# Layer-norm squares summed on VectorE, a group's squares issued one step earlier, and four low-part subtractions moved from GpSimd to VectorE

## The chip, the cores and the metric

One core of a Trainium2 chip runs the whole program. The metric is device time in microseconds (us): a launch from start to end, the median of several runs. The engines are named as in the profile: PE is the matrix engine (TensorE), DVE is VectorE, ACT is ScalarE, POOL is GpSimd, SP issues most of the DMA transfers. Each engine works through its own list of instructions in order and waits where an instruction needs a result that is not there yet.

## The reference, cut to what matters

The program is one inference step of a hybrid decoder on 336 tokens (8 running sequences of 8 tokens, 16 learned tokens, a prompt of 256), all in float32, with 1024 features. Two branches read one input projection, and a large expert layer follows:

```
xn   = rmsnorm(x);  proj = xn @ w_in + b_in          # 80 column blocks of 128
u    = ga * sigmoid(gb)                              # conformer branch
c    = silu(layernorm(causal_depthwise(u, 31 taps)))
y_a  = c @ w_conf_out + b_conf_out
xs, B, C, dt = ...                                   # Mamba-2 branch, 8 groups of 4 heads
y    = ssd(xs, dt, B, C, state) + D * xs
y    = group_rmsnorm(y * silu(z))                    # mean of squares per group
y_b  = y @ w_m_out
x    = x + (sigmoid(g_a) * y_a + sigmoid(g_b) * y_b) @ w_o
x    = x + peer(rmsnorm(x))                          # 16384 experts, 16 per head and token
```

Two of these steps are touched: the variance of the layer norm (a sum of squares over 1024 features, of which 128 lie on the partitions and 8 are tiles side by side) and the squares of each group for the grouped norm.

## The kernel before, in words

Activations lie with features on the 128 partitions and tokens along the row: a tile of 128 features by 336 tokens, eight tiles for 1024 features. Float32 products are formed from a high and a low part. `weight` (L234 to L243) loads a block of 128 x 1024 weights by DMA into `wraw`, ACT casts it to the high part `wh` (L211), and a subtraction `wraw - wh` gives the low part `wl` (L212). Which engine subtracts is set by a share `lm[0]`: with 0.05 one weight in twenty goes to DVE and the others to POOL. `proj` then runs 16 matmuls with `wh` and 8 with `wl`. There are two buffers each for `wh` and `wl`.

The first part of the program is a loop over eight groups `g`. In the turn of group `g + 1` the 128-column blocks of that group are projected, and between these projections the generator `ssd` of the group before is advanced, one `yield` at a time, so that its small matmuls lie between the large ones. Matmuls of this part are pinned: PE runs them in the order in which the code issues them. The other engines' orders are chosen by the scheduler at build time. The last steps of `ssd` are `update(0)`, `update(2)` (state sums, written back to HBM in `ssm_s`), and then the squares: two on ACT (L634), their sum on POOL (L635), a matmul `pgn` that sums over partitions, and an addition on DVE (L641).

In the turn of the last group (g = 7) the tasks are eight gate projections, the gates 0 to 7 below. After gate 0 comes `norm_mean` (L703): PE sums the convolution outputs, ACT scales the mean `rs` (L707), DVE subtracts it from eight tiles (L709), ACT squares them (L711) and POOL adds seven of them to the first (L713). Then comes gate 1, and behind it the `pgn` matmul of group 6. `norm_scale` (L717) follows gate 3: PE sums `squares[0]` over partitions, and `rstd_of` (L201 to L208, on DVE and ACT) makes the reciprocal root. After gate 7 the `conf_out` projections 0 to 7 use the normalised result, with other work between them: the squares of group 7 and, behind `conf_out(1)`, `gnorm_stats`, which turns the eight groups' sums into one bf16 operand on DVE (L201 to L222, tile `acs`). The matmuls `pgb` behind `conf_out(5)` spread this operand over the partitions, and DVE scales each group with it (L657).

After that come the projections with `w_m_out` and `w_o`, the query projection, the choice of experts, and two long loops over 128 blocks each of the two expert tables (L1180 and L1271), during which rows are also gathered one token at a time (L994).

Of the kernel before, what the change touches and what calls it, by code (L numbers as in the profile page):

```python
# [13 lines left out]
OP = mybir.AluOpType  # L14
# [31 lines left out]
HB = 64  # L46
KTILES = ((0, NGAT), (128, 128), (256, 64))
NU = (54, 28, 40)
LM = (0.05, 0.05, 0.1, 0.5)
CE = 1  # L50
LOW = 400
NW0 = 3
# [80 lines left out]
def body(tc, ia, oa, stop=None):  # L133
    nc = tc.nc
    with ExitStack() as top:
# [10 lines left out]
        def mm(*a_, **kw):  # L146
            i_ = nc.tensor.matmul(*a_, **kw)  # L147
            if pin[0]:
                tc.keep_in_program_order(i_)
# [26 lines left out]
        def V(name, j):  # L176
            o, n = VEC[name]
            return vec[:, o + j:o + j + 1]

        def C(name, rows=128):  # L180
            o, n = CST[name]
            if o < NCK:
                return cst[:rows, o:o + n]
            return cstm[0][:rows, o - NCK:o - NCK + n] if o < NCM else cstm[1][:rows, o - NCM:o - NCM + n]
# [6 lines left out]
        def act(out, in_, f, **kw):  # L191
            chain(nc.scalar.activation(out, in_, f, **kw))  # L192

        def pj(name="pj"):
            return ps.tile([128, PJ], F32, name=name, tag="pj", bufs=3)[:, :T]

        def rstd_of(dst, p, n, pool, tag="yo", load=True):
            r, c_ = dst.shape
            v = pool.tile([128, c_], F32, name="rsv", tag=tag, bufs=2)[:r]
            t = pool.tile([128, c_], F32, name="rst", tag=tag, bufs=2)[:r]  # L200
            nc.vector.tensor_scalar(v, p, 1.0 / n, EPS, op0=OP.mult, op1=OP.add)  # L201
            if load:
                chain(nc.scalar.preload_act_table_set("natural_log_exp_and_others"))
            act(t, v, AF.Ln)
            act(t, t, AF.Exp, scale=-0.5)
            nc.vector.scalar_tensor_tensor(v, v, -0.5, t, op0=OP.mult, op1=OP.mult)
            nc.vector.tensor_tensor(v, v, t, op=OP.mult)
            nc.vector.scalar_tensor_tensor(dst, v, 1.5, t, op0=OP.add, op1=OP.mult)  # L208
# [5 lines left out]
        def stack3(dst, src, n, pool, tag):  # L214
            r_ = pool.tile([128, T], F32, name="s3r", tag=tag, bufs=2)[:n]
            b_ = pool.tile([128, 2 * T], BF, name="s3b", tag=tag, bufs=2)[:n, :T]
            nc.vector.tensor_copy(dst[:n], src)
            nc.vector.tensor_tensor(r_, src, dst[:n], op=OP.subtract)
            nc.vector.tensor_copy(dst[H:H + n], r_)
            nc.vector.tensor_copy(b_, r_)  # L220
            nc.vector.tensor_tensor(r_, r_, b_, op=OP.subtract)
            nc.vector.tensor_copy(dst[2 * H:2 * H + n], r_)  # L222
# [4 lines left out]
        def proj(out, w, act, first=True, last=True):  # L227
            for k in range(KD):
                for c_ in range(2):
                    mm(out, w[0][:, k, :], act(k)[c_], start=(first and k == 0 and c_ == 0), stop=False)  # L230
            for k in range(KD):
                mm(out, w[1][:, k, :], act(k)[0], start=False, stop=(last and k == KD - 1))

        def weight(src, i):  # L234
            raw = wp.tile([128, KD, 128], F32, name="wraw", bufs=rb[0])
            nc.sync.dma_start(raw, src[i].rearrange("p (k m) -> p k m", m=128))
            h = wp.tile([128, KD, 128], F32R, name="wh", bufs=2)
            l = wp.tile([128, KD, 128], F32R, name="wl", bufs=2)
            nw[0] += 1
            f_ = lm[0]  # L240
            on_dve = int((nw[0] + 1) * f_) > int(nw[0] * f_)
            split(h, l, raw, on_pool=not on_dve, on_dve=lm[0] == 1)
            return h, l  # L243

        lm, nw = [LM[3]], [NW0]

# [3 lines left out]
        def misc(shape, name):  # L250
            return ps.tile(shape, F32, name=name, tag="misc", bufs=2)
# [240 lines left out]
        def ssd(g, xg, bc, sz):  # L492
            BT, CT = bc[:, 0, :], bc[:, 1, :]
            st = sp.tile([128, NQ, 256], F32, name="st", bufs=2)
# [89 lines left out]
            def update(q):  # L584
                pair_ = [misc([128, 512], "pst2"), ps.tile([128, PJ], F32, name="pst2", tag="pj", bufs=3)]
                for d_ in range(2):
                    for s_ in range(2):
                        t_ = slice(32 * s_, 32 * s_ + 32)
                        mm(pair_[s_][:, d_ * 256:(d_ + 1) * 256], Bm[t_, q + d_], wx[0][t_], start=True, stop=True)
                for s_ in range(2):  # L590
                    sv = st[:, 4 * s_ + q:4 * s_ + q + 2].rearrange("p q c -> p (q c)")
                    nc.vector.tensor_tensor(sv, sv, pair_[s_], op=OP.add)
# [33 lines left out]
            yield  # L626
            update(0)
            yield
            update(2)
            nc.sync.dma_start(oa["ssm_s"][g], st)  # L630
            yield
            sq = [tp.tile([128, T], F32, name="sq", bufs=4) for _ in range(2)]
            for b in range(2):
                nc.scalar.activation(sq[b], xg[:, b, :], AF.Square)  # L634
            nc.gpsimd.tensor_tensor(sq[0], sq[0], sq[1], op=OP.add)  # L635
            p = pj("pgn")[:G]
            mm(p, C("gsel")[:, g * G:(g + 1) * G], sq[0], start=True, stop=True)
            if g == 0:
# [5 lines left out]
        def gnorm_stats():  # L644
            r8 = tp.tile([128, T], F32, name="rs", bufs=2)[:G]
            rstd_of(r8, pgn, 256, tp, load=False)
            r24 = mp.tile([3 * H, T], BF, name="acs3", tag="acs3")
            nc.vector.memset(r24, 0.0)
            stack3(r24, r8, G, tp, "yo")
            return r24  # L650

        def gnorm(g, r24):
            p = ps.tile([128, T], F32, name="pgb", tag="y", bufs=2)
            mm(p, id3[:, g:g + 1].to_broadcast([3 * H, 128]), r24, start=True, stop=True)
            for b in range(2):
                y = ygf[g][:, b, :]
                nc.vector.scalar_tensor_tensor(y, y, V("m_norm", 2 * g + b), p, op0=OP.mult, op1=OP.mult)  # L657

        def gsplit(g):
            yh = pair(F32R, "yh")  # L660
            yl = m2.tile([128, 2, T], F32R, name="yl", bufs=8)
            for b in range(2):
                split(yh[:, b, :], yl[:, b, :], ygf[g][:, b, :], on_pool=b == 0)
            yg.append((yh, yl))
# [27 lines left out]
        def conf_out(j):  # L692
            ga = gates[j]
            act(ga, ga, AF.Sigmoid)
            w = weight(ia["w_co"], j)
            p = pj()
            proj(p, w, lambda k: (ch[:, k, :], cl[k]))
            nc.vector.scalar_tensor_tensor(ga, p, V("b_co", j), ga, op0=OP.add, op1=OP.mult)

        gates, squares, normed, r24 = [], [], [], []  # L700

        def norm_mean():
            pm = pj()  # L703
            mm(pm, ones, csum, start=True, stop=False)
            mm(pm, ones, cb[:, KD - 1, :], start=False, stop=True)
            mu = tp.tile([128, T], F32, name="rs", bufs=2)
            nc.scalar.mul(mu, pm, 1.0 / D)  # L707
            for k in range(KD):
                nc.vector.tensor_tensor(cb[:, k, :], cb[:, k, :], mu, op=OP.subtract)  # L709
                sq = tp.tile([128, T], F32, name="sq", bufs=4)  # L710
                nc.scalar.activation(sq, cb[:, k, :], AF.Square)  # L711
                if k:
                    nc.gpsimd.tensor_tensor(squares[0], squares[0], sq, op=OP.add)  # L713
                else:
                    squares.append(sq)

# [31 lines left out]
        for f in steps + zsteps:  # L748
            f()
        lm[0] = LM[0]  # L750
        pin[0] = True
        old = iter(())
        for g in range(G):
            new = ssd(g, *tiles, sz)
            if g + 1 < G:
                tiles, steps = xbc(g + 1)
                tasks = conf(g + 1) + steps
            else:
                lm[0] = LM[1]
                tasks = [gate] * 8  # L760
# [25 lines left out]

        m2 = mix.enter_context(tc.tile_pool(name="m2", bufs=1))
        r24.append(gnorm_stats())
        for j in range(2, 6):
            conf_out(j)  # L790
        for g in range(G):
            gnorm(g, r24[0])
            gsplit(g)
            if g % 2 and g < 4:
                conf_out(6 + g // 2)
        for _ in range(3):
            gate()
        pin[0] = False
        lm[0] = LM[2]
        mh = m2.tile([128, KD, T], F32R, name="mh")  # L800
# [15 lines left out]
        for j in range(KD):  # L816
# [11 lines left out]
            else:  # L828
                sq = tp.tile([128, T], F32, name="sq", bufs=4)
# [575 lines left out]
```

## Time and profile before

| | us |
|---|---|
| median of three runs (lowest to highest) | 1414.23 (1413.54 to 1415.16) |
| the profiled execution's own time | 1416.98 |
| its span in the trace | 1415.2 |
| busy: PE, DVE, POOL, ACT | 1327.6, 1011.0, 596.1, 526.2 |
| mean granted PE clock | 0.977 |

The trace counts from the start of the span. Groups 0 to 7 are projected until about 365 us. The gates, the layer norm, `conf_out` and the grouped norm fill 365 to 465 us, the output and query projections 465 to 640 us, and the expert layer the rest. A row of the timeline has a start, a duration, the engine, the line, the operation with its tiles, and in brackets how long the engine was idle before and what ended that. A row of the table by stretches has for each engine its busy time, then the granted PE clock (1.00 is full speed), the DMA share and GB/s. A row of the chain of waits has a start, a length and the work that the end of the program hung on at that time.

### The profile page before, as it was taken

The page shows a single profiled execution, that of the slowest core. Times are in us where ns is not written, and L with a number is a line of the kernel's source. Part 1 is how long each engine was busy: PE and PEld are TensorE (multiplying, and loading weights), DVE is VectorE, ACT ScalarE, POOL GpSimd, SP SyncE. Part 2 cuts the span into 40 slices and gives each one's busy share as a digit, 9 for nine tenths or more (in the row PEclk, how much of TensorE's full clock was granted, in tenths as well). Part 3 has the DMA queues.
Part 4 walks back from the last instruction along what each step waited for, and adds up shares of the span by engine and source line. Part 5 has one row for each costly group of instructions (what it writes and reads, how often), then busy time and mean ns, then how long its engine had stood idle before and what let it go on. Part 6 is the DMA issues. An engine that isn't in the chain of part 4 may idle for free.

```text
span 1415.2 us, 24492 instructions
## 1 busy us (share of the span) xinstructions
PE 1327.6 (94%) x9294; PEld 1257.4 (89%) x9294; DVE 1011.0 (71%) x2326; ACT 526.2 (37%) x1348; POOL 596.1 (42%) x490
## 2 busy tenths in 40 slices
PE   5899999999699999999999879999979999987997
PEld 3898889888588999989999879999979999987997
DVE  6787778877556434679999966777888787775423
ACT  4678776778564543533222221112110110111001
POOL 2267767767665755743212342223232222242100
PEclk9899999999899999999999999999989999999999
DMA  5435453445324344636999899999999999999983
GB/s 198 149 122 167 165 173 127 151 163 169 120 66 147 124 144 141 201 97 216 416 414 413 322 416 413 381 372 394 408 399 416 373 373 392 388 416 415 414 323 98
DMA packets 86806, 382.05 MB, mean 270 GB/s; under 512 B 10112, under 2 KB 15360, under 8 KB 66080
## 3 DMA queue, kind: packets, MB, share of 16 engines
q1 hardware_dynamic: 64144, 226.87, 44.7%
q0 software_dynamic: 20736, 151.00, 26.3%
q10 hardware_dynamic: 1808, 2.60, 0.5%
q8 instruction: 73, 1.20, 0.3%
q14 instruction: 45, 0.37, 0.1%
HBM read 367.41 MB, written 13.03 MB: 269 GB/s over the span
## 4 chain that ended last, share of the span: by engine, by line
PE 75%; DVE 13%; DMA 8%; ACT 2%; issue 1%; POOL 1%; DVEq 0%; SPq 0%; POOLq 0%; ACTq 0%
PE pj L147 31%; PE va L1271 19%; PE pj L1180 11%; PE pg L1209 4%; DMA eraw<-in_vE_dram 3%; DMA eraw<-in_uT_dram 3%; PE pst L147 2%; DVE ygat L1114 2%; DVE wuv L1106 2%; PE po L147 1%; PE pdec L147 1%; PE py L147 1%; PE ptr L152 1%; DMA nd<-x1d 1%; DVE si L916 1%
## 5 line engine op out<-in xcount | busy, mean ns | idle before, releaser
L994 POOL DMA_INDIRECT wuv<-in_peer_uv_dram,gid x144 | 184.1, 1279 | 510.9 <-DVE ygat L1114 193.0
L212 POOL TENSOR_TENSOR wl<-wraw,wh 128x1024 fp32r<-128x1024 f32 x115 | 276.6, 2406 | 185.4 <-ACT wh L211 111.7
L1180 PE MATMUL pj<-nd,eraw 128*128 128x176 f32 x2048 | 324.1, 318 | 13.3 <-DMA eraw<-in_uT_dram 10.0
L1180 PEld LDWEIGHTS pj<-nd,eraw 128*128 128x128 f32 x2048 | 311.3, 193 | 17.2 <-ACT S L1182 8.3
L1271 PE MATMUL va<-S,eraw 128*128 128x176 f32 x2048 | 314.9, 314 | 11.8 <-DMA eraw<-in_vE_dram 11.8
L1271 PEld LDWEIGHTS va<-S,eraw 128*128 128x128 f32 x2048 | 306.1, 190 | 16.4 <-DMA eraw<-in_vE_dram 14.7
L147 PE MATMUL pj<-ah,wh 128*128 128x336 f32 (+1 forms) x768 | 248.3, 332 | 2.4 <-ACT xnf L192 2.1
L147 PE MATMUL pj<-al,wh 128*128 128x336 f32 (+1 forms) x768 | 239.8, 320 | 0.0
L1114 DVE SCALAR_TENSOR_TENSOR ygat<-wuv,scg,ygat 128x1024 f32<-128x1024 f32 x128 | 164.0, 1281 | 56.0 <-ACT scg L1109 55.1
L1106 DVE SCALAR_TENSOR_TENSOR wuv<-wuv,x2m 128x1024 f32<-128x1024 f32 x128 | 156.1, 1219 | 37.7 <-DMA wuv<-in_peer_uv_dram,gid 37.7
L211 ACT CAST wh<-wraw 128x1024 fp32r<-128x1024 f32 x128 | 134.2, 1049 | 130.3 <-PE pj L147 79.0
L1108 ACT ACTIVATE scg<-scg 128x1 f32<-128x1 f32 x144 | 29.1, 202 | 402.7 <-DVE wuv L1106 391.8
L390 DVE SCALAR_TENSOR_TENSOR pcv<-ccat,vec,pcv 128x272 f32<-128x272 f32 x464 | 152.4, 393 | 18.0 <-ACT pcv L388 18.0
L147 PEld LDWEIGHTS pj<-ah,wh 128*128 128x128 f32 x768 | 147.1, 192 | 10.7 <-ACT xnf L192 3.9
L147 PEld LDWEIGHTS pj<-al,wh 128*128 128x128 f32 x768 | 147.1, 192 | 1.1 <-DVE al L212 0.5
L147 PE MATMUL pj<-ah,wl 128*128 128x336 f32 (+1 forms) x768 | 138.2, 318 | 0.0
L147 PEld LDWEIGHTS pj<-ah,wl 128*128 128x128 f32 x768 | 122.5, 188 | 0.8 <-issue 0.7
L1182 ACT ACTIVATE S<-pj 128x176 f32<-128x176 f32 x128 | 37.6, 311 | 156.0 <-PE pj L1180 155.9
L1209 PE MATMUL pg<-oh 128*128 128x64 bf16 x1056 | 75.5, 241 | 0.0
L1209 PEld LDWEIGHTS <-oh 128*128 128x128 bf16 x1056 | 71.1, 117 | 2.2
L1216 DVE TENSOR_TENSOR S<-S,pg 128x192 f32<-128x192 f32 (+1 forms) x66 | 31.7, 508 | 52.1 <-PE pg L1209 50.4
L405 DVE SCALAR_TENSOR_TENSOR pj<-mcat,vec,pj 128x360 f32<-128x360 f32 x96 | 57.0, 594 | 1.4 <-ACT pj L403 1.1
(353 smaller groups left out, 1704.4 us busy)
## 6 DMA issues: line engine op xcount, KB each, us to landing
eraw<-in_uT_dram SPq DMA_DIRECT2D x128, 512.0 KB
eraw<-in_vE_dram SPq DMA_DIRECT2D x128, 512.0 KB
wraw<-in_w_in_dram SPq DMA_DIRECT2D x80, 512.0 KB
st<-in_state_dram SPq DMA_DIRECT2D x8, 1024.0 KB
out_ssm_s_dram<-st SPq DMA_DIRECT2D x8, 1024.0 KB
wraw<-in_w_mo_dram SPq DMA_DIRECT2D x16, 512.0 KB
wraw<-in_w_q_dram SPq DMA_DIRECT2D x16, 512.0 KB
wraw<-in_w_co_dram SPq DMA_DIRECT2D x8, 512.0 KB
```

Source lines behind the costliest of these rows:

```text
L147: i_ = nc.tensor.matmul(*a_, **kw)
L211: (nc.vector.tensor_copy if on_dve else nc.scalar.copy)(h, src)
L212: (nc.gpsimd if on_pool else nc.vector).tensor_tensor(l, src, h.bitcast(F32), op=OP.subtract)
L390: t = nc.vector.scalar_tensor_tensor(o, i_, wv, a_, op0=OP.mult, op1=OP.add)
L405: nc.vector.scalar_tensor_tensor(o, cat[:, w:w + n], wv, o, op0=OP.mult, op1=OP.add)
L994: i_ = nc.gpsimd.indirect_dma_start(out=u, out_offset=None, in_=ia["peer_uv"], in_offset=bass.IndirectOffsetOnAxis(ap=gid[:, c:c + 1], axi ...
L1106: nc.vector.scalar_tensor_tensor(u[:, :D], u[:, :D], 1.0, x2m if c < NPICK else x2e, op0=OP.mult, op1=OP.mult, accum_out=w)
L1114: nc.vector.scalar_tensor_tensor(a_, u[:, D:], scg[:, c:c + 1], a_, op0=OP.mult, op1=OP.add)
L1180: i_ = nc.tensor.matmul(p[:, :ND], raw[:, k, :], nd[:, k, :], start=(k == 0), stop=(k == KD - 1))
L1182: nc.scalar.activation(Sv(b), p[:, :ND], AF.Gelu)
L1209: i_ = nc.tensor.matmul(pg[:, q, :], B[:, q // 4, :, q % 4], A[:, c_, q // 4, :, q % 4], start=(c_ == 0), stop=(c_ == 2))
L1271: i_ = nc.tensor.matmul(va[k // 2][:, k % 2], raw[:, k, :], Sv(b), start=False, stop=(b == 127), skip_group_check=True)
```

## The change

Three edits. The seven additions of the layer norm's squares go from POOL to DVE. In `ssd` the squares of a group and their sum are issued ahead of `update(2)`, in the same step as its state copy to HBM, and no longer one step later; the `pgn` matmul stays where it was on PE. And during `conf_out(2)` to `conf_out(5)` the share of low parts on DVE is 0.999, which is all four; before, it was 0.05, and by the count one of the four was on DVE already.

```diff
-LM = (0.05, 0.05, 0.1, 0.5)
+LM = (0.05, 0.05, 0.1, 0.5, 0.999)
...
             yield
             update(0)
             yield
-            update(2)
-            nc.sync.dma_start(oa["ssm_s"][g], st)
-            yield
             sq = [tp.tile([128, T], F32, name="sq", bufs=4) for _ in range(2)]
             for b in range(2):
                 nc.scalar.activation(sq[b], xg[:, b, :], AF.Square)
             nc.gpsimd.tensor_tensor(sq[0], sq[0], sq[1], op=OP.add)
+            update(2)
+            nc.sync.dma_start(oa["ssm_s"][g], st)
+            yield
             p = pj("pgn")[:G]
             mm(p, C("gsel")[:, g * G:(g + 1) * G], sq[0], start=True, stop=True)
...
                 if k:
-                    nc.gpsimd.tensor_tensor(squares[0], squares[0], sq, op=OP.add)
+                    nc.vector.tensor_tensor(squares[0], squares[0], sq, op=OP.add)
...
         r24.append(gnorm_stats())
+        lm[0] = LM[4]
         for j in range(2, 6):
             conf_out(j)
+        lm[0] = LM[1]
```

The orders of the built programs differ at few places. For groups 0 to 5 the squares stand where they stood on every engine. PE's order differs only in the loop over the first expert table, where at three places a run of 8 to 24 projection matmuls stands one to about 36 `pg` matmuls earlier or later, and DVE's and ACT's lists follow with a few rows.

POOL in the turn of the last group, from the end of group 6's output to the state scaling. Before (`wl` is a weight's low part, L713 the layer norm's sum, L635 the sum of group 6's squares, `wx` the scaled inputs of group 7):

```order
L582 TENSOR_TENSOR xg<-xg,sz 128x336
L212 TENSOR_TENSOR wl<-wraw,wh 128x1024 x2
L530 TENSOR_TENSOR wx_4562<-xt_4559,wd_202 80x256
L212 TENSOR_TENSOR wl<-wraw,wh 128x1024
L713 TENSOR_TENSOR sq<-sq 128x336 x7
L635 TENSOR_TENSOR sq<-sq 128x336
L530 TENSOR_TENSOR wx_4660<-xt_4657,wd_226 128x256
L530 TENSOR_TENSOR wx_4669<-xt_4666,wd_242 128x256
L212 TENSOR_TENSOR wl<-wraw,wh 128x1024
L562 TENSOR_TENSOR st<-st,el 128x256 x8
```

and with the change (the sum of group 6's squares is now L632):

```order
L582 TENSOR_TENSOR xg<-xg,sz 128x336
L212 TENSOR_TENSOR wl<-wraw,wh 128x1024
L632 TENSOR_TENSOR sq<-sq 128x336
L212 TENSOR_TENSOR wl<-wraw,wh 128x1024
L530 TENSOR_TENSOR wx_4567<-xt_4564,wd_202 80x256
L212 TENSOR_TENSOR wl<-wraw,wh 128x1024
L530 TENSOR_TENSOR wx_4660<-xt_4657,wd_226 128x256
L530 TENSOR_TENSOR wx_4669<-xt_4666,wd_242 128x256
L212 TENSOR_TENSOR wl<-wraw,wh 128x1024
L562 TENSOR_TENSOR st<-st,el 128x256 x8
```

The seven additions have left POOL, and the sum of group 6's squares stands three rows of weights and inputs earlier, behind the first of three low parts.

DVE at the same place, with the change, from the mean's subtraction (L709) to the reciprocal root of the layer norm (L201); before, the same rows stood there without the three of L713, and the memset (L648) behind the two rows of L527:

```order
L709 TENSOR_TENSOR cbuf<-cbuf,rs 128x336 x8
L641 TENSOR_TENSOR pgn<-pgn 8x336
L713 TENSOR_TENSOR sq<-sq 128x336
L648 MEMSET acs_5114 96x168
L527 TENSOR_TENSOR xt_4657<-ptr,dtok_218 128x256
L527 TENSOR_TENSOR xt_4666<-ptr,dtok_234 128x256
L713 TENSOR_TENSOR sq<-sq 128x336 x4
L540 TENSOR_TENSOR dec<-dec,pcb 80x4x80
L713 TENSOR_TENSOR sq<-sq 128x336 x2
L540 TENSOR_TENSOR dec<-dec,pcb 128x4x128
L548 COPY hs_4773<-pst 128x256
L201 TENSOR_SCALAR rsv<-pj 128x336
```

The first addition stands behind the addition of group 6's `pgn`, and the last two behind the product with `pcb`, a matmul that PE runs after gate 2.

DVE at `gnorm_stats`, from the sum of group 7's `pgn` to the operand of `pgb`. Before:

```order
L641 TENSOR_TENSOR pgn<-pgn 8x336
L201 TENSOR_SCALAR rsv<-pgn 8x336
L206 SCALAR_TENSOR_TENSOR rsv<-rsv,rst 8x336
...
L217 CAST acs_5114<-rs 8x336
L218 TENSOR_TENSOR s3r<-rs,acs_5114 8x336
L698 SCALAR_TENSOR_TENSOR ge<-pj,vec,ge 128x336
L219 CAST acs_5114<-s3r 8x336
L220 CAST s3b<-s3r 8x336
L221 TENSOR_TENSOR s3r<-s3r,s3b 8x336
L222 CAST acs_5114<-s3r 8x336
```

and with the change:

```order
L641 TENSOR_TENSOR pgn<-pgn 8x336
L201 TENSOR_SCALAR rsv<-pgn 8x336
L212 TENSOR_TENSOR wl<-wraw,wh 128x1024
L206 SCALAR_TENSOR_TENSOR rsv<-rsv,rst 8x336
...
L217 CAST acs_5114<-rs 8x336
L698 SCALAR_TENSOR_TENSOR ge<-pj,vec,ge 128x336
L212 TENSOR_TENSOR wl<-wraw,wh 128x1024
L218 TENSOR_TENSOR s3r<-rs,acs_5114 8x336
L219 CAST acs_5114<-s3r 8x336
L220 CAST s3b<-s3r 8x336
L221 TENSOR_TENSOR s3r<-s3r,s3b 8x336
L698 SCALAR_TENSOR_TENSOR ge<-pj,vec,ge 128x336
L222 CAST acs_5114<-s3r 8x336
```

The low parts of `conf_out(4)` and `conf_out(5)` now stand inside this sequence (that of `conf_out(2)` stands a little ahead of it and that of `conf_out(3)` was there before), and the evictions L698 have moved by a row. On POOL five low parts in a row behind the sum of group 7's squares have become two, those of `conf_out(6)` and `conf_out(7)`.

## The prediction

> **What bounds the kernel now.** I read three views, from coarse to fine. First the page's chain that ended last, which says whose work the end hangs on, and the table by stretches, which says where that holds.
>
> ```profile
> PE 75%; DVE 13%; DMA 8%; ACT 2%; issue 1%; POOL 1%; DVEq 0%; SPq 0%; POOLq 0%; ACTq 0%
> ```
>
> ```profile
> 370.00:390.00 20.00, 8.80 (x44) 6.14 (x43) 5.78 (x14) 9.91 (x27) 12.54 (x12) 0.70 0.33 106
> ...
> 430.00:450.00 20.00, 17.30 (x110) 16.35 (x109) 13.59 (x14) 12.21 (x16) 10.66 (x5) 0.99 0.54 178
> 450.00:470.00 20.00, 17.34 (x94) 16.48 (x94) 15.74 (x29) 9.67 (x20) 12.90 (x10) 0.84 0.26 86
> 470.00:520.00 50.00, 50.00 (x327) 50.00 (x326) 14.66 (x13) 22.45 (x31) 29.24 (x14) 1.00 0.46 143
> ...
> 900.00:1000.00 100.00, 100.00 (x824) 99.22 (x822) 76.00 (x115) 19.45 (x76) 25.62 (x21) 1.00 0.99 388
> 1200.00:1300.00 100.00, 88.17 (x628) 85.15 (x627) 70.38 (x94) 12.94 (x52) 29.59 (x23) 1.00 1.00 406
> ```
>
> The first busy column is PE. It is full from 470 us on until DVE and then the DMA engines (shares 0.99 and 1.00) take over in the expert layer. All of that begins with results of the stages ahead, so time won before 465 us moves the rest forward whole. The hole is at 370 to 390 us, with PE busy for 8.80 of 20 us, in the stage that the change edits. Then PE's waits from 355 to 640 us (total, times, longest), the two longest:
>
> ```profile
> PE pgn L147 <- POOL sq L635: 11.2, 1, 11.2
> PE pgb L147 <- DVE acs L222: 3.4, 1, 3.4
> ```
>
> Last, the timeline at the first of them, PE, then POOL, then ACT:
>
> ```profile
> 373.83 1.40 PE L147 MATMUL pj<-ah,wl 128*128 128x336 f32 x8
> 386.43 1.29 PE L147 MATMUL pgn<-sq,cstm 128*8 128x336 f32 x2 [11.20 <-POOL sq L635]
> ```
>
> ```profile
> 375.37 3.49 POOL L212 TENSOR_TENSOR wl<-wraw,wh 128x1024 fp32r<-128x1024 f32 x1 [3.68 <-ACT wh L211]
> 378.82 6.71 POOL L713 TENSOR_TENSOR sq<-sq 128x336 f32<-128x336 f32 x7
> 385.49 0.89 POOL L635 TENSOR_TENSOR sq<-sq 128x336 f32<-128x336 f32 x1
> ```
>
> ```profile
> 383.62 0.48 ACT L634 ACTIVATE sq<-xg 128x336 f32<-128x336 f32 x1 [0.49 <-POOL sq L713]
> ```
>
> PE ends gate 1 at 375.23 and then needs the squares of group 6. Their sum is queued on POOL behind a low part and the seven additions of the layer norm, and the squares themselves on ACT behind those of the layer norm, which wait for POOL to free a buffer.
>
> **Term 1: the wait for group 6's squares goes, 13.6 us.** With the change the sum stands behind one low part, ahead of `norm_mean`:
>
> ```profile
> 360.99 0.91 POOL L582 TENSOR_TENSOR xg<-xg,sz 128x336 f32<-128x336 f32 x1
> 362.97 2.37 POOL L212 TENSOR_TENSOR wl<-wraw,wh 128x1024 fp32r<-128x1024 f32 x1 [1.07 <-PE pj L147]
> ```
>
> Its input is complete at 361.9, the low part ends at 365.3, and the sum at 0.9 us is there by 366.3, 9 us before PE asks. What the same PE work takes without a wait stands in the chain at group 5's squares, up to `pq` of group 6, against `pq` of group 7 and the norm's matmul now:
>
> ```profile
> 331.85 0.66 PE pgn L147 x2
> ...
> 333.72 3.91 PE pj L147 x24
> 337.63 1.00 PE pq L147 x16
> ...
> 394.65 1.00 PE pq L147 x16
> ...
> 400.55 0.78 PE pj L147 x2
> ```
>
> From `pgn` to `pq` it was 337.63 - 331.85 = 5.78 us there; here it is 394.65 - 375.23 = 19.42 us from the end of gate 1. The difference, 13.6, is the wait of 11.2 and 2.4 us of work done at the half clock that follows it (granted 0.70 in this stretch). The other operands are ready: gate 2's low part was made before, and gate 3's ends at 375.37 + 3.49 = 378.86, ahead of its use. Bounds: 11.2, if the clock fell for another reason, and 13.6.
>
> **Term 2: the additions on DVE, a loss of 0.3 us.** PE needs `squares[0]` 5.90 us after `pq` starts (400.55 - 394.65), so now at 381.01 + 5.90 = 386.9. Before, the sum was ready at 385.5 for a use at 400.5; that cover is gone. DVE has no such addition in the trace. The nearest row is a subtraction of two 128x336 tiles in SBUF, 0.51 us:
>
> ```profile
> L212 DVE TENSOR_TENSOR ml<-gs,mh x4: 507/508/510, 490.1 to 555.6; 128x336 fp32r<-128x336 f32 x4
> ```
>
> Seven cost 3.6 us, where DVE is nearly idle. But a DVE operation on two SBUF tiles waits while POOL is in one, as `rs` did, at 2.58 us here and 0.52 at the program's start (chain, third row):
>
> ```profile
> 405.34 2.58 DVE L208 SCALAR_TENSOR_TENSOR rs<-rsv,rst 128x336 f32<-128x336 f32 x1
> 405.15 2.40 POOL L212 TENSOR_TENSOR wl<-wraw,wh 128x1024 fp32r<-128x1024 f32 x1 [0.21 <-ACT wh L211]
> 16.92 0.52 DVE rs L208
> ```
>
> So I put the list of front's second DVE block on the clock, with POOL's pieces:
>
> ```profile
> 373.22 3.44 DVE L709 TENSOR_TENSOR cbuf<-cbuf,rs 128x336 f32<-128x336 f32 x8 [2.22 <-ACT rs L707]
> 389.39 1.25 POOL L530 TENSOR_TENSOR wx<-xt,wd 128x256 f32<-128x256 f32 x2 [3.01 <-DVE xt L527]
> 397.12 4.62 POOL L562 TENSOR_TENSOR st<-st,el 128x256 f32<-128x256 f32 x8
> ```
>
> L709 ends at 376.7, the `pgn` addition at 377.2. Addition 1 waits for gate 3's low part (378.9) and ends at 379.4; `xt` takes until 380.2; additions 2 and 3 let one L530 (0.6) pass each, until 382; number 4 may meet gate 4's low part, until 384.2; 5 lets one L562 (0.58) pass, 385.2; then the product with `pcb`, and 6 and 7 with an L562 each, 387.2. That is 0.3 late. Bounds: no loss, if POOL's pieces fall between, and 4.8 us, if two more low parts of 2.4 get ahead.
>
> **Term 3: the layer norm's root, a loss of 0.4 us.** POOL's state scaling and the low parts of gates 5 and 6 come some 0.4 us later against PE, since additions get between. The root's three steps meet them as now, and PE's wait behind them grows from 1.00 to 1.4:
>
> ```profile
> 410.37 0.70 PE L147 MATMUL pst<-wx,xt 128*128 128x256 f32 x2 [1.00 <-DVE dec L540]
> ```
>
> Bounds: the wait vanishes (gain 1.0), or one more low part is in the way (loss 2.4).
>
> **Term 4: low parts on DVE, a gain of 0.5 us.** The wait of 3.4 us at `pgb` is this (DVE, POOL, ACT, PE, and from the chain the projection behind it):
>
> ```profile
> 442.72 2.57 DVE L219 CAST acs<-s3r 8x336 bf16<-8x336 f32 x1
> ...
> 450.33 0.33 DVE L222 CAST acs<-s3r 8x336 bf16<-8x336 f32 x1
> 442.70 7.24 POOL L212 TENSOR_TENSOR wl<-wraw,wh 128x1024 fp32r<-128x1024 f32 x3 [3.84 <-ACT wh L211]
> 441.58 1.98 ACT L211 CAST wh<-wraw 128x1024 fp32r<-128x1024 f32 x2
> 446.15 1.05 ACT L211 CAST wh<-wraw 128x1024 fp32r<-128x1024 f32 x1 [2.59 <-issue]
> 450.71 0.72 PE L147 MATMUL pgb<-acs,id 96*128 96x336 bf16 x2 [3.41 <-DVE acs L222]
> 451.43 6.07 PE pj L147 x24
> ```
>
> Three small DVE steps (0.3 to 0.5 us alone, as L222) each wait out one POOL low part of 2.4 us. The change takes the first of the three, that of `conf_out(5)`, and puts it into DVE's list instead, at 1.22 us (half of POOL's 2.40 above):
>
> ```profile
> L212 DVE TENSOR_TENSOR wl<-wraw,wh x13: 1204/1223/1866, 14.1 to 643.6; 128x1024 fp32r<-128x1024 f32 x13
> ```
>
> Cast by 442.6, it ends at 443.8, L218 at 444.3. Then POOL, whose weight 6 is cast at 443.6, takes its turn to 446.5, L219 waits, L220 and L221 end at 447.6. Weight 7 is cast at 447.2, so POOL's last low part starts about 447.6, while DVE evicts L698, and L222 waits for it until 450.2, against 450.7 now: 0.5 us gained. PE is at `pgb` at 447.3, so a wait of 2.9 stays. Bounds: nothing, and 5.8: the whole 3.4, with the 2.4 us by which the projection behind it (6.07) exceeds 3.7 us at full clock. The low part of `conf_out(2)` delays two state sums by 1.3 us, which only the copy to HBM waits for; that of `conf_out(4)` fills a gap in which DVE waits for ACT. What stands behind costs nothing on PE.
>
> [...]
>
> ```profile
> 609.66 0.33 PE L899 MATMUL px<-cst,xe 128*128 128x128 f32 x1 [2.48 <-POOL xe L897]
> 613.00:616.00 3.00, 3.00 (x12) 3.00 (x13) 3.00 (x20) 0.30 (x2) 0.00 (x0) 0.50 0.03 5
> ```
>
> So at 2.9 I keep the half clock.
>
> **Term 5: the expert loops, 0.** Three runs of matmuls moved there; PE and DMA are full either way (900 to 1000 us). Bounds: 2 us to each side.
>
> **Sum.** 13.6 - 0.3 - 0.4 + 0.5 = 13.4 us. The profiled execution took 1416.98, of which 1415.2 are its span; it would take 1403.6. The median of the runs lies 2.75 under it: 1400.8 us.
>
> **The rivals.** (a) The root of the group norm gets through: L219 to L222 pass between POOL's low parts and PE does not wait at `pgb`. Then term 4 is 5.8 and the time 1395.5. For it: POOL has two low parts left for four steps. Against it: both are cast at just the wrong moments. Chance 0.22.
>
> (b) The wait at `pgb` stays near 2.9 but the clock does not fall: 2.4 more, 1398.4. [...] Chance 0.07, since the shorter wait at 609 us did halve it.
>
> (c) A new wait at the norm's matmul: the additions lose the turn to two more low parts, 4.5 us more than in term 2, and the half clock costs 2.4: 1407.7. For it: my list ends within 0.3 us of the need. Against: only two low parts are due there. Chance 0.08.
>
> (d) Slower. The moved runs in the first expert loop break the rhythm of table blocks, gathers and `pg`, and the DMA engines, the bound from 800 to 1300 us, run at 388 GB/s in place of 406: 500 x (406/388 - 1) = 23 us, so 1424. It turns the result once it costs 16.2 us, 3.2% of these 500. Against it: three runs only, and both rates occur in the loops already. Chance 0.03.
>
> (e) The change does nothing on the clock: the wait only changes its place, to another operand behind `pgn`. 1414. I see no operand that is late there. Chance 0.03.
>
> **How the numbers follow.** The forecast has 0.57; its own range is 1398.5 to 1403.5, from terms 2, 3 and 5. With (a) and (b) that makes 0.86 between 1394 and 1405, which is the range. What this measurement can tell from no change is about 0.2%, 2.8 us: faster are the forecast, (a), (b) and (c), 0.94; the same (e), 0.03; slower (d), 0.03.
>
> **What would show it.** In the new profile PE should have no wait at group 6's `pgn`, `pq` of group 7 should start near 381 us, and the granted clock from 370 to 390 should be 1.00. The norm's matmul near 387 shows term 2: a wait there for DVE's L713 of over 1 us makes it (c). L222 should still end some 2.9 us after `conf_out(5)`; if PE does not wait at `pgb`, it is (a). From `pgb` to the end the span should keep its length within 2 us; if it grows by more than 16, it is (d). A `pgn` wait of 5 us or more would make the prediction wrong.

## The result and the profile after

| us | before | changed |
|---|---|---|
| median of four runs (lowest to highest) | 1414.42 (1413.54 to 1415.16) | 1401.87 (1398.62 to 1403.79) |
| ratio, with its 95% interval | | 0.9909 (0.9893 to 0.9925) |
| the profiled execution's own time | 1416.98 | 1403.79 |
| its span | 1415.2 | 1402.0 |
| mean granted PE clock | 0.977 | 0.982 |

The forecast was 1400.8, with a range from 1394 to 1405. The profiled executions lie 13.2 us apart, the medians 12.55; the sum of the terms was 13.4. In the changed kernel the sum of a group's squares is L632, and lines behind `gnorm_stats` have numbers two higher (the first expert loop's L1180 is L1182).

First the shares of the chain that ended last, of the changed kernel, and its table by stretches, with the same columns as before (PE is the first busy column; behind the five engines stand the granted clock, the DMA share and GB/s):

```profile
PE 76%; DVE 13%; DMA 8%; ACT 2%; issue 1%; POOL 0%; DVEq 0%; SPq 0%; ACTq 0%
```

```profile
370.00:390.00 20.00, 19.83 (x128) 16.49 (x127) 16.30 (x26) 14.27 (x33) 13.88 (x15) 1.00 0.41 132
...
430.00:450.00 20.00, 15.46 (x89) 14.49 (x88) 16.38 (x26) 8.62 (x15) 12.23 (x7) 0.91 0.34 106
...
900.00:1000.00 100.00, 100.00 (x841) 99.28 (x840) 79.65 (x123) 19.73 (x76) 25.91 (x20) 1.00 1.00 398
1200.00:1300.00 100.00, 86.52 (x583) 82.97 (x581) 63.16 (x79) 12.43 (x50) 32.85 (x23) 1.00 1.02 416
```

The hole at 370 to 390 us is filled: PE is busy for 19.83 of 20 us in place of 8.80, at a granted clock of 1.00 in place of 0.70. The expert loops look as they did, and the chain's shares are within a point of the old ones. Then PE's waits from 355 to 640 us, those that the prediction spoke of:

```profile
PE pgb L147 <- DVE acs L222: 2.8, 1, 2.8
...
PE pst L147 <- DVE dec L540: 2.1, 1, 2.1
...
PE pj L147 <- DVE sq L713: 0.2, 1, 0.2
```

The `pgn` wait of 11.2 us is gone, a new one of 0.2 us stands at the norm's matmul, the one behind the layer norm's root has doubled from 1.0 to 2.1 us, and the one at `pgb` went from 3.4 to 2.8 us. The timeline of PE gives the places:

```profile
373.67 1.40 PE L147 MATMUL pj<-ah,wl 128*128 128x336 f32 x8
375.01 0.73 PE L147 MATMUL pgn<-sq,cstm 128*8 128x336 f32 x2
...
380.79 1.07 PE L147 MATMUL pq<-st,gs 128*32 128x256 f32 x16
...
387.19 0.83 PE L147 MATMUL pj<-sq,cst 128*128 128x336 f32 x2 [0.17 <-DVE sq L713]
...
398.23 0.70 PE L147 MATMUL pst<-wx,xt 128*128 128x256 f32 x2 [2.14 <-DVE dec L540]
...
450.23 0.30 PE L147 MATMUL pgb<-acs,id 96*128 96x336 bf16 x1 [0.65 <-DVE xg L657]
```

The last row is the last `pgb` matmul, a good mark for the end of the stage. In the kernel before it stands here:

```profile
464.08 0.30 PE L147 MATMUL pgb<-acs,id 96*128 96x336 bf16 x1 [0.65 <-DVE xg L657]
```

Up to the mark the program became 464.08 - 450.23 = 13.85 us shorter. Behind it the span has 1402.0 - 450.23 = 951.8 us, against 1415.2 - 464.08 = 951.1 before. So all of the gain was made ahead of the mark, and 0.7 us were given back behind it.

The gain up to the mark splits into these pieces, by the timeline where nothing else is said. Gate 1 ends at 373.67 + 1.40 = 375.07, which is 0.16 earlier than before. From there to `pq` it is 380.79 - 375.07 = 5.72 us now and was 394.58 - 375.23 = 19.35: 13.63 won. From `pq` to the norm's matmul it is 387.19 - 380.79 = 6.40 and was 5.90: 0.50 lost, of which the listed wait is 0.17. The wait at the `pst` matmul lost 2.14 - 1.00 = 1.14. At `pgb` the wait is 2.81 in place of 3.41, and `pgb` and the projection behind it, in the chain of waits of the changed kernel, take 0.45 + 5.24 in place of 0.72 + 6.07:

```profile
437.97 0.45 PE pgb L147 x2
438.41 5.24 PE pj L147 x24
```

which is 0.6 + 1.1 = 1.7 won. The sum is 0.16 + 13.63 - 0.50 - 1.14 + 1.7 = 13.85, that of the mark.

### The profile page after: what moved, and what is told of

The parts are those of the page before. It is cut to its first block, busy times and chain, and to the rows that moved or that the text cites. A ratio compares the mean times of both kernels' runs of the same rounds, so it can differ in the third digit from the quotient of the medians.

```text
span 1402.0 us, 24488 instructions
## 1 busy us (share of the span) xinstructions
PE 1326.0 (95%) x9294; PEld 1256.3 (90%) x9294; DVE 1020.2 (73%) x2336; ACT 525.3 (37%) x1348; POOL 578.4 (41%) x480
## 4 chain that ended last, share of the span: by engine, by line
PE 76%; DVE 13%; DMA 8%; ACT 2%; issue 1%; POOL 0%; DVEq 0%; SPq 0%; ACTq 0%
PE pj L147 31%; PE va L1273 19%; PE pj L1182 12%; PE pg L1211 4%; DMA eraw<-in_vE_dram 4%; PE pst L147 2%; DVE ygat L1116 2%; DVE wuv L1108 2%; DMA eraw<-in_uT_dram 2%; PE po L147 1%; PE pdec L147 1%; PE py L147 1%; DMA nd<-x1d 1%; DMA wuv<-in_peer_uv_dram,gid 1%; PE ptr L152 1%
## 5 line engine op out<-in xcount | busy, mean ns | idle before, releaser
L996 POOL DMA_INDIRECT wuv<-in_peer_uv_dram,gid x144 | 178.7, 1241 | 516.7 <-DVE ygat L1116 206.6
L212 POOL TENSOR_TENSOR wl<-wraw,wh 128x1024 fp32r<-128x1024 f32 x112 | 269.2, 2405 | 184.7 <-ACT wh L211 101.9
L1182 PE MATMUL pj<-nd,eraw 128*128 128x176 f32 x2048 | 324.1, 318 | 8.5 <-DMA eraw<-in_uT_dram 5.5
L1182 PEld LDWEIGHTS pj<-nd,eraw 128*128 128x128 f32 x2048 | 311.6, 193 | 12.4 <-ACT S L1184 7.7
```

Of the source, the lines that this page charges most:

```text
L212: (nc.gpsimd if on_pool else nc.vector).tensor_tensor(l, src, h.bitcast(F32), op=OP.subtract)
L996: i_ = nc.gpsimd.indirect_dma_start(out=u, out_offset=None, in_=ia["peer_uv"], in_offset=bass.IndirectOffsetOnAxis(ap=gid[:, c:c + 1], axi ...
L1182: i_ = nc.tensor.matmul(p[:, :ND], raw[:, k, :], nd[:, k, :], start=(k == 0), stop=(k == KD - 1))
```

## The experiments

Ratios are against runs of the kernel before on the same chip, with a 95% interval. The mark is the start of the last `pgb` matmul in the profile, the rest what the span has behind it.

| kernel | median, us | ratio (interval) | mark, us | rest, us |
|---|---|---|---|---|
| squares early alone | 1411.49 | 0.998 (0.9962 to 0.9998) | 460.61 | 949.8 |
| additions on DVE alone | 1412.43 | 0.9989 (0.9971 to 1.0007) | 457.58 | 953.2 |
| low parts on DVE alone | 1414.97 | 1.0005 (0.9991 to 1.0019) | 462.36 | 950.7 |
| the change, again | 1403.23 | 0.9918 (0.9892 to 0.9944) | 451.96 | 950.0 |
| six low parts | 1396.42 | 0.9872 (0.9839 to 0.9904) | 445.80 | 953.7 |
| all low parts | 1400.72 | 0.9898 (0.9861 to 0.9934) | 445.96 | 952.8 |
| the change, third time | 1403.03 | 0.9922 (0.9894 to 0.995) | 450.51 | 952.6 |
| two edits, no low parts | 1403.42 | 0.9917 (0.99 to 0.9933) | 450.30 | 951.8 |
| gates from 4 | 1395.78 | 0.9857 (0.9841 to 0.9874) | 443.86 | 952.4 |
| six low parts, again | 1398.81 | 0.9877 (0.9856 to 0.9898) | 449.02 | 952.4 |

The first four kernels ran on one chip, the next three on another, and the last three together again. The rest varies by 4 us between profiles, also between three of the same kernel (951.8, 950.0, 952.6), so the mark is the finer measure of this stage. It needs one caution. In six kernels (additions alone, low parts alone, two edits, all low parts, gates from 4, six low parts again) a stretch of 3.4 us at a granted clock of 0.50 begins at the mark or within 1.4 us of it, behind the last short waits of the stage (1.30 and 0.65 us), and it costs at most 1.7 us, half its length, that the mark doesn't count. Where that matters the start of the first `psc` matmul is given too, the first of the choice of experts: 609.8 us before and 596.0 in the first profile of the change.

### One edit at a time

**Squares early alone.** Only the order in `ssd` is changed; the additions stay on POOL and the low parts where they were.

```diff
-            update(2)
-            nc.sync.dma_start(oa["ssm_s"][g], st)
-            yield
             sq = [tp.tile([128, T], F32, name="sq", bufs=4) for _ in range(2)]
             for b in range(2):
                 nc.scalar.activation(sq[b], xg[:, b, :], AF.Square)
             nc.gpsimd.tensor_tensor(sq[0], sq[0], sq[1], op=OP.add)
+            update(2)
+            nc.sync.dma_start(oa["ssm_s"][g], st)
+            yield
```

> Only the second edit: the squares of a group and their sum ahead of update(2); the layer norm's additions and the low parts stay on POOL. Theory (the two first edits need one another): PE no longer waits at group 6's pgn, but POOL's seven additions (0.96 us each), now among two low parts and the state scaling, end some 10 us after the norm's matmul wants them, so the wait moves there; 1410 to 1413 us. Rival (moving the sum is enough, the additions on VectorE are decoration): no wait of over 1 us at either place, 1401 to 1403 us.

The median fell by 3.6 us (1415.08 on this chip to 1411.49). PE's waits, POOL's timeline and PE's timeline of this kernel, one row of each:

```profile
PE pj L147 <- POOL sq L713: 10.0, 1, 10.0
```

```profile
394.30 2.83 POOL L713 TENSOR_TENSOR sq<-sq 128x336 f32<-128x336 f32 x3
```

```profile
397.19 1.49 PE L147 MATMUL pj<-sq,cst 128*128 128x336 f32 x2 [9.98 <-POOL sq L713]
```

The wait at `pgn` is gone, but one of 10.0 us has appeared further on, at the norm's matmul: POOL's last additions end at 397.13, and the matmul starts at 397.19. The same seven additions that held up group 6's squares now hold up the layer norm itself.

**Additions on DVE alone.** Only the engine of L713 is changed.

```diff
-                    nc.gpsimd.tensor_tensor(squares[0], squares[0], sq, op=OP.add)
+                    nc.vector.tensor_tensor(squares[0], squares[0], sq, op=OP.add)
```

> Only the first edit: the seven additions on VectorE, the squares of group 6 still behind the layer norm's on ScalarE. Theory: the wait at pgn shrinks from 11.2 to 6 to 8 us, since ScalarE's squares of group 6 still stand behind eight squares that wait for buffers which VectorE's additions free; 1408 to 1411 us. Rival (the additions on GpSimd alone were the cause): the wait is under 1.5 us, 1401 to 1403 us.

The median fell by 2.65 us, not to be told from no change by the interval; the mark is 6.5 us earlier, the first `psc` 5.0. The time lies above the 1408 to 1411 us expected, as the wait of 8.6 us does above its 6 to 8. PE's longest wait in the stage, and ACT's timeline ahead of it:

```profile
PE pgn L147 <- POOL sq L635: 8.6, 1, 8.6
```

```profile
378.77 2.32 ACT L711 ACTIVATE sq<-cbuf 128x336 f32<-128x336 f32 x4 [2.51 <-DVE sq L713]
381.22 1.09 ACT L634 ACTIVATE sq<-xg 128x336 f32<-128x336 f32 x2
```

POOL is free of the additions, and still PE waits 8.6 us for group 6's squares. ACT makes them (L634) only behind the layer norm's squares (L711), and those wait for a buffer that DVE's additions free. So group 6's squares stood in two lists behind the layer norm, POOL's and ACT's, and this edit clears one of them.

**Low parts on DVE alone.** Only the share of low parts around `conf_out(2)` to `conf_out(5)` is changed.

```diff
-LM = (0.05, 0.05, 0.1, 0.5)
+LM = (0.05, 0.05, 0.1, 0.5, 0.999)
...
+        lm[0] = LM[4]
         for j in range(2, 6):
             conf_out(j)
+        lm[0] = LM[1]
```

> Only the third edit: low parts of conf_out(2) to (5) on VectorE. Theory: the wait at pgb shrinks from 3.4 to 2.9 us, since GpSimd's last two low parts still block the first and the last step of the root; 1413.5 to 1414.5 us. Rival: VectorE's small steps get through and the wait goes, 1408 to 1410 us.

The median is 1414.97, 0.1 us below the kernel before. Its waits:

```profile
PE pgn L147 <- POOL sq L635: 10.8, 1, 10.8
PE pgb L147 <- DVE acs L222: 2.8, 1, 2.8
```

The wait at `pgb` falls from 3.4 to 2.8 us, as in the whole change; the hole ahead of it stays. The mark is 464.08 - 462.36 = 1.7 us earlier, but a stretch at half clock from 463.7 on follows it, and the first `psc`, at 609.6, is only 0.2 earlier, which fits the median.

**The change, again,** without an edit, on the same chip.

> The changed kernel again, beside the others on one chip. Theory: 1400 to 1403 us, and what its runs differ by arises in the expert loops, so the stretch up to the last pgb matmul is as long as in the first profile (450.2 us) within 0.3 us. Rival: the spread of its runs comes from the edited stage, where the half clock comes or not: then that stretch differs by 1 to 3 us.

The median is 1403.23, 11.85 us below the kernel before on this chip. By the medians the three edits alone add up to 3.6 + 2.65 + 0.1 = 6.4 us. By the marks they add up to 3.5 + 6.5 + 1.7 = 11.7 of 13.85, and by the first `psc` matmul, behind the stretches at half clock, to 3.5 + 5.0 + 0.2 = 8.7 of 13.8. So a part of the gain belongs to no edit by itself, as the early squares and the moved additions need one another, but its size is only roughly known, 2 to 5.5 us. The mark, though, was expected within 0.3 us of the first profile's 450.23 and came at 451.96. Of these 1.73 us, 0.38 are there ahead of the `pst` matmul (398.61 against 398.23). The other 1.35 arise behind the wait at it. In this profile:

```profile
398.61 0.96 PE L147 MATMUL pst<-wx,xt 128*128 128x256 f32 x2 [2.14 <-DVE dec L540]
```

```profile
400.00:402.00 2.00, 2.00 (x15) 1.67 (x12) 1.82 (x5) 2.00 (x4) 1.36 (x1) 0.50 0.00 0
```

and in the first one:

```profile
400.00:402.00 2.00, 2.00 (x15) 1.87 (x14) 1.49 (x5) 2.00 (x4) 1.74 (x2) 1.00 0.00 0
```

The wait is 2.14 us in both, but here a granted clock of 0.50 follows it and there 1.00.

**Two edits, no low parts.** The whole change without its third edit:

```diff
         r24.append(gnorm_stats())
-        lm[0] = LM[4]
         for j in range(2, 6):
             conf_out(j)
-        lm[0] = LM[1]
```

> The first two edits without the third. Theory (the third is worth 0.5 us): wait at pgb 3.4 us in place of 2.8, the rest as in the changed kernel; 1401 to 1404 us. Rival (the third edit is worth more together with the others): 1405 us or more.

The median is 1403.42, 12.2 us below the kernel before, and the mark 450.30 against 450.23 with the third edit. The wait at `pgb` and the projection behind it (waits, and chain):

```profile
PE pgb L147 <- DVE acs L222: 3.4, 1, 3.4
```

```profile
438.14 0.72 PE pgb L147 x2
438.85 4.87 PE pj L147 x24
```

Wait, `pgb` and projection take 3.4 + 0.72 + 4.87 = 9.0 us here, and 2.8 + 0.45 + 5.24 = 8.5 us with the third edit. The marks show only 0.07, as this profile was 0.4 us ahead from group 6 on (its `pq` of that group starts at 336.99, against 337.41). So the edit is worth near 0.5 us in one pair of profiles, less than the times can tell from nothing.

### The two waits that are left

**Six low parts.** The prediction held that the wait at `pgb` stays because POOL has two low parts left, those of `conf_out(6)` and `conf_out(7)`. Here they go to DVE too (edit against the changed kernel):

```diff
         for j in range(2, 6):
             conf_out(j)
-        lm[0] = LM[1]
...
+        lm[0] = LM[1]
         for _ in range(3):
             gate()
```

> The changed kernel with the low parts of conf_out(2) to (7) on VectorE, so that GpSimd has none while the root of the group norm is made. Theory (GpSimd's last two low parts hold L219 and L222): the wait at pgb falls from 2.8 us to under 0.5 and the projection behind it runs at full clock, 3.7 instead of 5.2 us; about 4 us less than the changed kernel, 1397 to 1400 us. Rival (the low part of conf_out(6), now ahead of L222 on VectorE, takes GpSimd's place): the wait stays over 1.5 us, and the time is that of the changed kernel.

Waits and chain of this kernel:

```profile
PE pst L147 <- DVE dec L540: 2.1, 1, 2.1
...
PE pgb L147 <- DVE acs L222: 0.2, 1, 0.2
```

```profile
435.56 3.68 PE pj L147 x24
```

The wait fell from 2.8 to 0.2 us, and the projection from 5.24 to 3.68: 4.2 us, and the mark moved by 450.23 - 445.80 = 4.4, of which 0.27 lay ahead of the `pst` matmul. L219 and L222 now take 0.33 us each. POOL's last two low parts were what held up the root. The wait at `pst` is untouched, as it lies ahead of the edit.

**All low parts.** Behind the wait at `pst` are POOL's low parts of the gates. Here those of all eight gates go to DVE, added to the edit above:

```diff
-                lm[0] = LM[1]
+                lm[0] = LM[4]
```

(ahead of the list of eight gate projections)

> As six_lowparts, and the low parts of the last group's eight gates on VectorE too. Theory (the layer norm's root is late since GpSimd's low parts of gates 5 and 6 block it): PE's wait of 2.1 us for dec (L540) falls under 1 us, and that of 0.2 us for the squares stays under 0.5; 1 to 3 us less than six_lowparts, 1395 to 1398 us. Rival (VectorE becomes the bound there, with 10 us more of work): new waits of PE for VectorE of 2 us or more between 370 and 430 us, and no gain over six_lowparts.

The wait at `pst` is gone, but the mark is 445.96, no earlier than with six. DVE's and PE's timeline show what took its place:

```profile
368.97 1.22 DVE L212 TENSOR_TENSOR wl<-wraw,wh 128x1024 fp32r<-128x1024 f32 x1
...
372.84 0.27 DVE L390 SCALAR_TENSOR_TENSOR cbuf<-ccat,vec,pcv 128x64 f32<-128x64 f32 x1
```

```profile
373.16 0.83 PE L147 MATMUL pj<-cbuf,cst 128*128 128x336 f32 x2 [2.02 <-DVE cbuf L390]
```

The first gates' low parts now stand on DVE among the last steps of the convolution, and `norm_mean`'s matmul waits 2.02 us for these. One wait of 2.1 us was exchanged for one of 2.0. The 1 to 3 us that the theory promised over six low parts did not come: the median is 4.3 us above that kernel's, with overlapping intervals. That is the outcome of the rival.

**The change, third time,** beside these two.

> The changed kernel as the yardstick of this chip: 1400 to 1404 us; waits of 2.8 us at pgb and 2.1 us at dec as before, with the half clock behind one or both of them, so that the last pgb matmul starts between 450 and 452 us.

Median 1403.03, mark 450.51, the wait at `pgb` 2.8. Against it, six low parts win 6.6 us by the medians on this chip, and 4.7 us by the marks; the intervals of the two ratios overlap by 0.001.

**Gates from 4.** If the low parts of the first gates are in the way on DVE and those of the later ones on POOL, only gates 4 to 7 should move:

```diff
             for n, f in enumerate(tasks):
+                if g + 1 == G and n == 4:
+                    lm[0] = LM[4]
                 f()
```

(with the edit of six low parts)

> As six_lowparts, and the low parts of the gates 4 to 7 on VectorE too, those of the gates 0 to 3 as before on GpSimd, so that VectorE finishes the convolution ahead of the mean as in the kernel before. Theory (GpSimd's low parts of gates 4 to 6 hold the additions and the root): no wait of 2.0 us at the mean, PE's waits for the squares and for dec under 0.3 us together, the last pgb matmul at 443.5 us in place of 445.8; 1393 to 1396 us. Rival: VectorE is late with another operand, and PE keeps over 1.5 us of waits between 370 and 430 us; 1396 to 1398 us.

A stretch of this kernel over the whole of the layer norm, and a step of its root from DVE's timeline:

```profile
366.00:400.00 34.00, 34.00 (x231) 29.71 (x230) 28.66 (x52) 23.65 (x50) 17.59 (x16) 1.00 0.38 125
```

```profile
391.58 0.51 DVE L207 TENSOR_TENSOR rsv<-rsv,rst 128x336 f32<-128x336 f32 x1
```

PE is busy for all 34 us at full clock, and the mark is 443.86, 6.4 us ahead of the change as it was given. With a median of 1395.78, 0.9857 of the kernel before, this version beats both kernels: its interval (to 0.9874) ends below those of the change on this chip (from 0.9894).

**Six low parts, again,** on the chip of the one above.

> six_lowparts again, as the yardstick for gates_from_4 on one chip: 1395 to 1399 us, last pgb matmul at 445.8 us, plus up to 1.7 where the half clock follows the 2.1 us wait for dec.

Median 1398.81, mark 449.02. That is 3.2 us later than the same kernel's first profile, more than the 1.7 allowed for: here too the wait of 2.14 us at `pst` is followed by the half clock, as in the second profile of the change, but for 6.8 us in place of 3.4 (398.2 to 405.0). So between six low parts and gates from 4 the medians are 3.0 us apart with overlapping intervals. That gates from 4 is the better one rests on its trace: it has no wait at `pst` and no half clock there. Its mark flatters it, as it has 3.4 us at half clock from 443.6 on, which the first profile of six low parts doesn't have: the first `psc` starts at 591.1, against 591.6 and 596.3 in the two profiles of six.

## Why the prediction was right, point by point

**Term 1, the wait for group 6's squares: 13.6 predicted, 13.63 measured.** The mechanism is shown by both sides. Group 6's sum now stands on POOL behind the one low part, and is there at 366.06, 9 us ahead of its use at 375.01 (the lower two rows are needed further on):

```profile
362.81 2.37 POOL L212 TENSOR_TENSOR wl<-wraw,wh 128x1024 fp32r<-128x1024 f32 x1 [1.08 <-ACT wh L211]
365.14 0.92 POOL L632 TENSOR_TENSOR sq<-sq 128x336 f32<-128x336 f32 x1
...
375.21 2.69 POOL L212 TENSOR_TENSOR wl<-wraw,wh 128x1024 fp32r<-128x1024 f32 x1 [3.68 <-ACT wh L211]
...
389.86 2.65 POOL L212 TENSOR_TENSOR wl<-wraw,wh 128x1024 fp32r<-128x1024 f32 x1
```

and with either half of the cure alone a wait of 8.6 to 10.0 us remained. The higher bound was the right choice: the 2.4 us of half clock went with the wait (granted 1.00 from 370 to 390).

**Term 2, the additions on DVE: a loss of 0.3 predicted, 0.50 measured.** The size was nearly right: 0.17 us are the wait for the last addition, and the rest comes at PE's `pcb` and what stands behind it, as PE's load of `pcb`'s operand waits 0.27 us for DVE's L540, which stands behind the fifth addition. These are DVE's rows of the changed kernel:

```profile
373.07 5.62 DVE L709 TENSOR_TENSOR cbuf<-cbuf,rs 128x336 f32<-128x336 f32 x8 [2.22 <-ACT rs L707]
...
379.03 0.49 DVE L713 TENSOR_TENSOR sq<-sq 128x336 f32<-128x336 f32 x1
...
385.78 1.35 DVE L713 TENSOR_TENSOR sq<-sq 128x336 f32<-128x336 f32 x2
...
388.13 0.51 DVE L201 TENSOR_SCALAR rsv<-pj 128x336 f32<-128x336 f32 x1
...
390.30 2.58 DVE L207 TENSOR_TENSOR rsv<-rsv,rst 128x336 f32<-128x336 f32 x1
...
393.75 3.83 DVE L726 TENSOR_TENSOR cbuf<-cbuf,rs 128x336 f32<-128x336 f32 x4
```

I had L709 end at 376.7, with gate 3's low part behind it. It ended at 378.7, because POOL's low part (375.21, in 2.69 us) got in between its eight steps: the seventh took 2.68 us, the others 0.50. My list had the same low part hold up the first addition instead, so that addition ended at 379.52, where I had 379.4, and the last ones at 385.78 + 1.35 = 387.13, where I had 387.2. DVE waits once for this low part either way; that the place did not matter was luck.

**Term 3, the layer norm's root: a loss of 0.4 predicted, 1.14 measured.** This term was mis-sized, within its bound of 2.4. The step that failed is "some 0.4 us later against PE": the low part of gate 5 came 1.45 us later against L201, which follows PE's norm matmul. POOL's state scaling ahead of it (L562) took 5.67 us in place of 4.62 and began later too. What counts is where POOL's low part of gate 5 falls against DVE's root. Before, from DVE's and POOL's timeline:

```profile
401.42 0.51 DVE L201 TENSOR_SCALAR rsv<-pj 128x336 f32<-128x336 f32 x1 [0.41 <-PE pj L147]
```

```profile
401.70 2.40 POOL L212 TENSOR_TENSOR wl<-wraw,wh 128x1024 fp32r<-128x1024 f32 x1
```

There it starts 0.28 us after L201, runs while the root is on ACT, and costs L206 about 1 us (1.47 in place of 0.51). Now it starts 389.86 - 388.13 = 1.73 us after L201. So L207, which takes 0.51 us with POOL out of the way (in gates from 4), takes 2.58 us, 2.1 lost in place of 1. Gate 6's low part cost about 2.1 us both times: before it held L208 (2.58), now L726, which stands ahead of the `dec` that PE waits for, with four steps in 3.83 us against 1.76. The meeting did not stay "as now"; gate 5's low part moved out of the time in which the root is on ACT, and that is the 1.1 us.

**Term 4, low parts on DVE: a gain of 0.5 predicted, 1.7 in the two profiles, about 0.5 by the experiment.** The wait of 2.8 us was predicted as 2.9, with the right cause: L219 and L222 waiting out the two low parts that POOL keeps, which the six low parts confirm by taking them away. In the changed kernel:

```profile
432.17 2.42 DVE L219 CAST acs<-s3r 8x336 bf16<-8x336 f32 x1
...
435.97 1.95 DVE L222 CAST acs<-s3r 8x336 bf16<-8x336 f32 x1
```

The projection of 5.24 against 6.07 us was not in the term. The kernel with two edits has 4.87 there and no third edit, so this part of the gain is not shown to be the edit's: the clock behind one and the same wait differed between profiles (below). The half clock that I kept behind this wait came in all three profiles of the change, behind 2.8 us: the projection took 5.24, 5.09 and 4.97 us there, against 3.68 at full clock in six low parts. It is partly luck that the sum, 13.4, came so close to the 13.85 of the mark: the 1.2 us by which this term came out higher made up for the 0.9 by which terms 2 and 3 lost more.

**Term 5, the expert loops: 0 predicted, 0.7 lost in the first profiles.** Three profiles of the change have 950.0 to 952.6 behind the mark and the kernel before 951.1, so no effect is seen.

**The rivals.** (a), the root getting through, did not happen in the change; what the end of the wait is worth shows when POOL's last two low parts go, 4.2 us beyond the change, against the 5.3 that I gave it (5.8 less 0.5). (b), no half clock at `pgb`, did not happen. (c), a new wait at the norm's matmul, came to a wait of 0.17 us, and a long wait at that place is possible: squares early alone has it at 10.0. (d) and (e) are out: the rest kept its length, and the stage became 13.85 us shorter.

## What to carry to other kernels

When a late operand stands behind the same work in the lists of two engines, clearing one list moves the wait and wins little (3.6 and 2.65 us here by the medians) and clearing both wins all of it (12): follow the operand back through every engine before costing an edit. After taking a wait away, put the neighbours' lists on the clock again, since which of the small steps meets a long instruction changes, and with it the cost (DVE's L207 took 0.51 us alone and 2.58 beside a low part of POOL's). Judge an edit that is worth under 3 us by its waits in several profiles, because the same wait of 2.14 us was followed by a granted clock of 1.00 in one profile and of 0.50 in another, and the marks of six low parts lay 3.2 us apart in two profiles.

## What the runs showed that I had not expected

**The clock behind a wait is not set by the wait's length alone.** I had kept the half clock at 2.9 us because 2.48 us was followed by it. In the profiles of these programs the same length goes both ways. The wait of 2.14 us at `pst` was followed by the full clock in four profiles (the first and third of the change, the first of six low parts, two edits; granted 1.00 from 400 to 402 us) and by the half clock in two (the second of the change and of six low parts; 0.50 there). The wait of 3.41 us at `pgb` was followed by the half clock before (a projection of 6.07 us), in squares early alone (5.24) and in two edits (4.87), but not in the kernel with the additions on DVE alone:

```profile
446.89 0.45 PE L147 MATMUL pgb<-acs,id 96*128 96x336 bf16 x2 [3.41 <-DVE acs L222]
```

```profile
447.33 3.68 PE pj L147 x24
```

Two of the stretches at half clock in the kernel before:

```profile
378.10:391.75 13.65, 5.32 (x19) 3.35 (x20) 1.54 (x4) 5.50 (x11) 9.03 (x11) 0.50 0.12 38
449.77:456.60 6.83, 5.89 (x22) 5.76 (x22) 4.22 (x9) 1.56 (x3) 1.07 (x2) 0.50 0.32 110
```

The one behind `pgb` in the changed kernel is 3.41 us long (438.80 to 442.21); 6.83 is twice that and 13.65 four times. A stretch of 3.41 us at half clock costs at most 1.7 us, half its length; the second profile of the change lost 1.35 us in one, from its `pst` matmul to its first `pgb` matmul. What decides which clock follows a wait of a given length, and what ends a stretch at half clock, these profiles don't show. A sum that hangs on it needs both clocks as bounds.

**Whether DVE or POOL loses the time varies.** In the kernel before, DVE's eight L709 ran through in 3.44 us and POOL's low part beside them took 3.49; in the changed kernel they took 5.62 and the low part 2.69, although the low part began 2.15 us after L709 in the one and 2.14 in the other. In additions on DVE alone L709 takes 5.58. So before it was POOL that lost time, 1.1 us over the 2.40 of its other low parts, and now it is DVE, 2.2 us over its 3.44. L207 shows the second case too: 2.58 us beside a low part in the changed kernel, and 0.51 without one in gates from 4. That DVE waits for POOL, as the prediction has it, is thus one of two cases. Who is next when one of several steps ends isn't shown by these runs; a sum that hangs on it needs both cases as bounds.
